# The gate projection of ten pairs of blocks with seven block products in place of eight, in a hybrid encoder block on one core

## The chip, the cores and the metric

The kernel runs on one core of a Trainium2 chip. The core has five engines with a queue of instructions each: TensorE (PE, matrix products, with its weight loads shown apart as PEld), VectorE (DVE), ScalarE (ACT), GpSimd (POOL) and SyncE (SP), which here only starts transfers. Each engine works through its queue in order, and semaphores hold an instruction back until what it needs is there. The metric is the time of one launch on the device in microseconds.

## The reference, cut to what matters

A layer mixes tokens (stick-breaking attention beside gated linear attention) and then applies a gated MLP. The change lies in the MLP. All of it is float32, for 512 tokens (SEQ), width 1024 (D) and inner width 2816 (FF):

```python
hn = _rmsnorm(h, norm_ffn_pre[l])
up = hn @ w_ffn_up[l]
act = jax.nn.gelu(_causal_dwconv(up, conv_w[l], conv_b[l]), approximate=True)
ffn = (act * (hn @ w_ffn_gate[l])) @ w_ffn_down[l]
h = h + _rmsnorm(ffn, norm_ffn_post[l])
```

The convolution goes over three tokens, one filter for each inner channel.

## The kernel before, in words

A float32 product is made of three passes: each operand is split into a high part (rounded to the float32r type that PE takes) and a low part (what is left), and PE adds high by high, high by low and low by high in PSUM. ACT makes the high part with a cast (L89 for weights, L137 elsewhere), and the low part is a subtraction, on POOL for weights of the projections (L90, in `load_w`) and on DVE elsewhere (L138, in `split`).

The normalised input of the MLP lies transposed in SBUF as `h2h` and `h2l` (high and low), eight tiles of 128 channels by 514 tokens; L207 makes the last low part. The inner width is 22 blocks of 128 (m), taken in eleven pairs p. For each block:

- the up projection: SP loads a 512 KB block of weights (`raw_up`) into one of three buffers with the tag raw, ACT casts, POOL subtracts, and PE runs 48 matmuls of 256 or 258 columns (L110, in `proj`) into `pt_up`;
- the convolution: ACT scales (L946), DVE adds the two other taps, a large and a tiny instruction for each (L949, L950), ACT applies gelu (L951);
- the gate projection: a load, a cast and a subtraction like those of up, then 24 matmuls of 512 columns (L958) into `ga`; for the first two blocks 48 of 256;
- the multiplication of the two, DVE (L961, and L963 for the odd block).

The down projection afterwards is a 2 x 2 block product done with seven products (p1, p5, p6, p3, p7, p4, p2, each 66 matmuls of 512 columns, L1020, in `product`). Its left operands are blocks of the MLP's inner activations, the half of blocks with even m and the half with odd m, each in two halves of 256 tokens: A11 and A12 are the even and the odd block for the first half of the tokens, and so on, and S1 to S4 are their sums and differences. DVE makes them at the end of each pair (L965 to L970). A11 and S1 are split at once, into `A11` and `S1`; S2, A12, A22, S4 and S3 are kept in float32 in `As` and split only when a product needs them (`late_split`, tile names `sh_p`, `sl_p`). The right operands are weights: `raw_p` for the first chunks of p1, `tw` (to which DVE adds `raw_t` and then `tv` while p1, p5 and p6 run, L1041) and `tv`. Their loads are on SP's queue.

The order on each engine is not written out: the source gives each instruction a rank, a scheduler that simulates the time line puts the instructions in order at build time, and `issue_after` pins a few of them. Buffers come free when their last reader is done.

Of the kernel before, what the change touches and what calls it, by code (L numbers as in the profile page):

```python
# [50 lines left out]
def block_kernel(ctx: ExitStack, tc: tile.TileContext, x, meta_tokens, norm_mix_pre, w_in, w_gk_up, b_gk,  # L51
# [884 lines left out]
    with tc.tile_pool(name="pu", bufs=2) as pu:  # L936
        for m in range(FT):
            pt = proj(load_w(cols(w_up, m * P), KT, f"up{m}", into=wx if m % 2 else None), h2h, h2l, FFNS, f"up{m}", apart=m < 2)
            if m % 2 == 0:
                yp = pu.tile([P, 3, HT], F32, tag="yp", name=f"yp{m}", bufs=1)  # L940
                y = yp[:, 0:2, :].rearrange("p s t -> p (s t)")
                dst = y
            else:
                y = pu.tile([P, SEQ], F32, tag="y", name=f"cy{m}", bufs=1)
                dst = As[:, A12 : A22 + 1, m // 2, :]
# [5 lines left out]
            last_gelu = act.activation(y, y, AF.Gelu_apprx_tanh)  # L951
# [8 lines left out]
            if m % 2 == 0:  # L960
                dve.tensor_tensor(out=dst, in0=pg_, in1=y, op=ALU.mult)  # L961
# [210 lines left out]
```

## Time and profile before

| | us |
|---|---|
| median of three runs | 971.16 (970.26 to 971.66) |
| profiled execution, its time | 969.08 |
| profiled execution, its span | 967.3 |
| MLP, up and gate (first up matmul 604.58, first down matmul 850.46) | 245.9 |
| down (850.46 to the end of the span) | 116.8 |

A row of a timeline has the start and the duration in us, the engine, the line, the operation, output<-inputs and the shape. A row of a group has the line, the engine, the shapes and a count, then the busy time in us and the mean of one in ns, then the idle time in front of these instructions and what ended it. Matmul durations overlap, so their pace is read from starts. A row of stretches has the length, then for each engine the busy time and the number of instructions (PE, PEld, DVE, ACT, POOL), the granted clock of PE, the share of the DMA engines' time and GB/s.

### The profile page before, as it was taken

What the parts mean: (1) busy time and instruction counts of PE and PEld (TensorE: products, weight loads), DVE (VectorE), ACT (ScalarE), POOL (GpSimd) and SP (SyncE); (2) the same over time, 40 slices, a digit from 0 to 9 for tenths busy, and PEclk for the clock granted to TensorE, in tenths of its full rate; (3) what the DMA queues carried; (4) which work ended last, traced back from release to release, by engine and by line L of the source; (5) the groups of instructions that cost most, each with busy time, mean ns of one, the idle gap of its engine ahead of it and who ended that gap; (6) DMA issues with size and microseconds to landing.
All of it is one profiled execution on the core that took longest, in us unless ns stands there. A gap on an engine that the chain in (4) does not pass through costs nothing.

```text
span 967.3 us, 16621 instructions
## 1 busy us (share of the span) xinstructions
PE 938.5 (97%) x6588; PEld 866.3 (90%) x6588; DVE 661.5 (68%) x1110; ACT 488.9 (51%) x913; POOL 357.6 (37%) x268
## 2 busy tenths in 40 slices
...
GB/s 216 45 66 66 66 45 66 66 66 44 67 66 67 86 68 45 65 88 58 75 55 90 117 207 140 61 112 93 89 92 104 87 88 94 103 237 167 254 86 127
DMA packets 129727, 92.79 MB, mean 96 GB/s; under 512 B 4064, under 2 KB 114914, under 8 KB 129650
## 3 DMA queue, kind: packets, MB, share of 16 engines
...
## 4 chain that ended last, share of the span: by engine, by line
PE 83%; DVE 10%; issue 2%; ACT 2%; POOL 2%; DMA 1%; DVEq 0%; ACTq 0%; POOLq 0%
PE pt_up L110 13%; PE ga L958 13%; PE pt_gr L110 5%; PE pt_gv L110 5%; PE pt_go L110 4%; PE pt_mg L110 4%; PE dA L1020 3%; PE pt_ms L110 3%; PE dD L1020 3%; PE pt_gk L110 2%; PE dB L1020 2%; PE wo L892 2%; PE pt_gq L110 2%; PE pt_sv L110 2%; PE pt_sk L110 2%
## 5 line engine op out<-in xcount | busy, mean ns | idle before, releaser
L90 POOL TENSOR_TENSOR wl_up<-raw_up,wh_up 128x1024 fp32r<-128x1024 f32 x22 | 53.0, 2409 | 68.3 <-ACT wh_up L89 68.3
L90 POOL TENSOR_TENSOR wl_ga<-raw_ga,wh_ga 128x1024 fp32r<-128x1024 f32 x22 | 55.2, 2509 | 56.6 <-ACT wh_ga L89 56.6
L110 PE MATMUL pt_up<-h2l,wh_up 128*128 128x256 f32 (+1 forms) x352 | 73.6, 283 | 0.3 <-DVE h2l L207 0.2
L110 PE MATMUL pt_up<-h2h,wh_up 128*128 128x256 f32 (+1 forms) x352 | 73.6, 283 | 0.2
L110 PE MATMUL pt_up<-h2h,wl_up 128*128 128x256 f32 (+1 forms) x352 | 73.3, 282 | 0.0
L958 PE MATMUL ga<-h2h,wl_ga 128*128 128x512 f32 (+1 forms) x192 | 72.2, 376 | 0.0
L958 PE MATMUL ga<-h2l,wh_ga 128*128 128x512 f32 (+1 forms) x192 | 72.2, 376 | 0.0
L958 PE MATMUL ga<-h2h,wh_ga 128*128 128x512 f32 (+1 forms) x192 | 72.0, 375 | 0.0
L89 ACT CAST wh_up<-raw_up 128x1024 fp32r<-128x1024 f32 x22 | 23.0, 1049 | 85.8 <-PE pt_up L110 76.2
L110 PEld LDWEIGHTS pt_up<-h2h,wh_up 128*128 128x128 f32 x352 | 56.9, 189 | 2.2 <-ACT h2h L206 0.5
L110 PEld LDWEIGHTS pt_up<-h2l,wh_up 128*128 128x128 f32 x352 | 55.5, 189 | 0.7 <-DVE h2l L207 0.7
L110 PEld LDWEIGHTS pt_up<-h2h,wl_up 128*128 128x128 f32 x352 | 55.3, 189 | 0.0
L958 PEld LDWEIGHTS ga<-h2h,wl_ga 128*128 128x128 f32 x192 | 36.2, 189 | 7.0
L949 DVE SCALAR_TENSOR_TENSOR cy<-pt_up,cw,cy 128x511 f32<-128x511 f32 (+1 forms) x22 | 16.4, 745 | 37.7 <-ACT cy L946 37.7
L958 PEld LDWEIGHTS ga<-h2l,wh_ga 128*128 128x128 f32 x192 | 36.2, 188 | 6.2
L958 PEld LDWEIGHTS ga<-h2h,wh_ga 128*128 128x128 f32 x192 | 36.2, 189 | 6.1
L949 DVE SCALAR_TENSOR_TENSOR yp<-pt_up,cw,yp 128x511 f32<-128x511 f32 (+1 forms) x22 | 16.4, 745 | 30.9 <-ACT yp L946 30.9
L89 ACT CAST wh_ga<-raw_ga 128x1024 fp32r<-128x1024 f32 x22 | 23.0, 1048 | 25.3 <-PE ga L958 24.8
L1048 POOL DMA_DIRECT2D tv<-in_w_ffn_down_dram x6 | 7.1, 1183 | 68.1 <-DVE wl_p L138 68.1
L90 POOL TENSOR_TENSOR wl_gr<-raw_gr,wh_gr 128x1024 fp32r<-128x1024 f32 x8 | 19.0, 2372 | 35.9 <-ACT wh_gr L89 33.1
L137 ACT CAST sh_p<-As 128x512 fp32r<-128x512 f32 (+1 forms) x30 | 17.4, 583 | 29.3 <-PE dB L1020 12.5
L90 POOL TENSOR_TENSOR wl_gv<-raw_gv,wh_gv 128x1024 fp32r<-128x1024 f32 x7 | 16.9, 2416 | 38.0 <-ACT wh_gv L89 38.0
...
## 6 DMA issues: line engine op xcount, KB each, us to landing
raw_up<-in_w_ffn_up_dram SPq DMA_DIRECT2D x22, 512.0 KB, 3.9
raw_ga<-in_w_ffn_gate_dram SPq DMA_DIRECT2D x22, 512.0 KB, 3.8
raw_t<-in_w_ffn_down_dram SPq DMA_DIRECT2D x10, 512.0 KB, 7.3
raw_gv<-in_w_in_dram SPq DMA_DIRECT2D x8, 512.0 KB, 3.9
raw_gr<-in_w_in_dram SPq DMA_DIRECT2D x8, 512.0 KB, 3.9
raw_mg<-in_w_in_dram SPq DMA_DIRECT2D x8, 512.0 KB, 3.9
raw_go<-in_w_gla_out_dram SPq DMA_DIRECT2D x8, 512.0 KB, 4.1
raw_ms<-in_w_in_dram SPq DMA_DIRECT2D x8, 512.0 KB, 4.0
```

Of the source, the lines that this page charges most:

```text
L89: act.copy(hi_out, raw)
L90: lo_eng.tensor_tensor(out=lo_out, in0=raw, in1=f32(hi_out), op=ALU.subtract)
L110: pe.matmul(dst, a[:, k, :], b[:, k, lo:hi], start=n == 0, stop=n == len(steps) - 1)
L137: act.copy(hi, src)
L892: pe.matmul(d0[i], m[k][:, t], w, start=k == 0 and q == 0, stop=k == 7 and q == 2)
L949: dve.scalar_tensor_tensor(out=y[:, d:], in0=pt[:, : SEQ - d], scalar=c, in1=y[:, d:], op0=ALU.mult, op1=ALU.add)
L958: pe.matmul(pg_[:, lo:hi], a[:, k, :], b[:, k, lo:hi], start=lo == 0 and k == 0 and q == 0, stop=k == KT - 1 and q == 2, skip_group_check= ...
L1020: mm[i] = pe.matmul(dsts[i], a, b, start=first and k == 0 and j == 0, stop=last and k == NP - 1 and j == 2, skip_group_check=True)
L1048: return lambda n, q, nk: pool.dma_start(out=t[:, q : q + nk, :], in_=block(s, c, q, nk), accum_op=ALU.add)
```

## The change

Pairs 1 to 10 no longer compute two gate blocks of 24 matmuls of 512 columns. The pair's gate product, 256 output channels by 512 tokens over 1024 input channels, is taken as a 2 x 2 by 2 x 2 block product with seven products of 12 matmuls of 256 columns (`times`, L1032). Four of the right operands are sums of quarters of h2 (`G`), computed once after pair 0 and split; three are quarters of h2. The left operands are quarters of the weights (l11, l21, l12, l22) and four sums of them (t1 to t4, `total`, L1052, on DVE). A pair's weights now come as two loads of 512 KB, each with both blocks for half of the input channels, into the raw buffers, which the sums and the splits of the quarters read. The seven splits are casts of 128x512 on ACT (L1023) and subtractions (L1024), five on DVE and two (l11, l12) on POOL.

The products are accumulated in three quarters of PSUM: a, e and g. Two of them are used for more than one sum, so e gets p1 added in place by DVE (L1067) after product t2, and ACT keeps copies (p1 L1062, u2 L1068, r5 L1071). DVE then forms two differences (d2, L1075 and L1080) and the two multiplications (L1079, L1081). Pair 0 is done as before.

The operands A12, A22 and S4 are no longer kept in SBUF: each pair's are written to HBM (`asd`) from ACT's queue, and read back into `back` (three loads of 1.44 MB) on SP's queue in the down stage. `hb` moves to another pool. The convolution and the operands go into functions with the same work in them.

```diff
-    pf = p3.enter_context(tc.tile_pool(name="pf", bufs=1))
-    hb = pf.tile([P, 4, D], F32, name="hb")
     dr = ctx.enter_context(tc.tile_pool(name="dr", bufs=1, space=bass.MemoryType.DRAM))
     hbd = dr.tile([4, P, D], F32, name="hbd")
+    asd = dr.tile([P, 3, FT // 2, SEQ // 2], F32, name="asd")
...
-    S2, A12, A22, S4, S3 = range(5)
-    As = pq.tile([P, 5, NP, HT], F32, name="As")
+    S2, S3 = range(2)
+    As = pq.tile([P, 2, NP, HT], F32, name="As")
...
+    pg = p3.enter_context(tc.tile_pool(name="pg", bufs=1, side="right"))
+    G = pg.tile([P, 4, 2, KH, HT], F32R, name="G")
...
+        def operands(p, yp, ys):
+
+            dve.tensor_tensor(out=yp[:, 2, :], in0=yp[:, 1, :], in1=ys[:, 1, :], op=ALU.subtract)
+            for o, i in ((A11, 0), (S1, 2)):
+                split(o[:, 0, p, :], o[:, 1, p, :], yp[:, i, :])
+            dve.tensor_tensor(out=As[:, S3, p, :], in0=yp[:, 0, :], in1=yp[:, 1, :], op=ALU.subtract)
+            dve.tensor_tensor(out=As[:, S2, p, :], in0=yp[:, 2, :], in1=yp[:, 0, :], op=ALU.subtract)
+            dve.tensor_tensor(out=ys[:, 2, :], in0=As[:, S2, p, :], in1=ys[:, 0, :], op=ALU.add)
+            act.dma_start(asd[:, :, p, :], ys)
...
-            for lo, hi in ((0, 256), (256, 512)) if m < 2 else ((0, 512),):
+            for lo, hi in ((0, 256), (256, 512)):
                 for k in range(KT):
                     for q, (a, b) in enumerate(((wh, h2h), (wh, h2l), (wl, h2h))):
                         pe.matmul(pg_[:, lo:hi], a[:, k, :], b[:, k, lo:hi], start=lo == 0 and k == 0 and q == 0,
                                   stop=k == KT - 1 and q == 2, skip_group_check=True)
-            if m % 2 == 0:
-                dve.tensor_tensor(out=dst, in0=pg_, in1=y, op=ALU.mult)
-                continue
-            dve.tensor_tensor(out=dst, in0=pg_.rearrange("p (s t) -> p s t", s=2), in1=y.rearrange("p (s t) -> p s t", s=2), op=ALU.mult)
-            p = m // 2
-            dve.tensor_tensor(out=yp[:, 2, :], in0=yp[:, 1, :], in1=As[:, A22, p, :], op=ALU.subtract)
-            for o, i in ((A11, 0), (S1, 2)):
-                split(o[:, 0, p, :], o[:, 1, p, :], yp[:, i, :])
-            dve.tensor_tensor(out=As[:, S3, p, :], in0=yp[:, 0, :], in1=yp[:, 1, :], op=ALU.subtract)
-            dve.tensor_tensor(out=As[:, S2, p, :], in0=yp[:, 2, :], in1=yp[:, 0, :], op=ALU.subtract)
-            dve.tensor_tensor(out=As[:, S4, p, :], in0=As[:, S2, p, :], in1=As[:, A12, p, :], op=ALU.add)
+            dve.tensor_tensor(out=y, in0=pg_, in1=y, op=ALU.mult)
+        operands(0, yp, ys)
...
+        K1, K2, N1, N2 = slice(0, KH), slice(KH, KT), slice(0, HT), slice(HT, SEQ)
+        with tc.tile_pool(name="py", bufs=1, reuse_waits="tile") as py:
+
+            def both(k, n, nm):
+                t = py.tile([P, KH, HT], F32, name=f"r{nm}")
+                dve.tensor_tensor(out=t, in0=f32(h2h[:, k, n]), in1=f32(h2l[:, k, n]), op=ALU.add)
+                return t
+
+            r12, r22 = both(K1, N2, "12"), both(K2, N2, "22")
+            dve.tensor_tensor(out=r22, in0=r12, in1=r22, op=ALU.subtract)
+            split(G[:, 0, 0], G[:, 0, 1], r22)
+            r11 = both(K1, N1, "11")
+            dve.tensor_tensor(out=r22, in0=r22, in1=r11, op=ALU.subtract)
+            split(G[:, 1, 0], G[:, 1, 1], r22)
+            dve.tensor_tensor(out=r12, in0=r11, in1=r12, op=ALU.subtract)
+            split(G[:, 2, 0], G[:, 2, 1], r12)
+            r21 = both(K2, N1, "21")
+            dve.tensor_tensor(out=r21, in0=r22, in1=r21, op=ALU.add)
+            split(G[:, 3, 0], G[:, 3, 1], r21)
+
...
+        def in_parts(src, nm, lo_eng=dve):
+
+            if place[1] == 0:
+                home, n = ((wx, 2), (wx, 2), (pt_, 1))[place[2] % 3]
+                place[2] += 1
+                place[0] = [home.tile([P, 2, KH, P], F32R, tag=t, name=f"{t}_{nm}", bufs=n) for t in ("wh", "wl")]
+            hi, lo = (t[:, place[1]] for t in place[0])
+            place[1] = 1 - place[1]
+            act.copy(hi, src)
+            lo_eng.tensor_tensor(out=lo, in0=src, in1=f32(hi), op=ALU.subtract)
+            return hi, lo
...
+        for p in range(1, NP):
+            c = slice(2 * p * P, 2 * p * P + 2 * P)
+            raw = []
+            for k in range(2):
+                r = wp.tile([P, KH, 2 * P], F32, tag="raw", name=f"raw_ga{p}_{k}")
+                sp.dma_start(r, w_gate[k * KH * P : (k + 1) * KH * P, c].rearrange("(k p) m -> p k m", p=P))
+                raw.append(r)
+            l11, l21, l12, l22 = (r[:, :, i * P : i * P + P] for r in raw for i in range(2))
+
+            def total(nm, a, b):
+                t = pt_.tile([P, KH, P], F32, tag=nm, name=f"{nm}_{p}")
+                dve.tensor_tensor(out=t, in0=a, in1=b, op=ALU.add)
+                return t
+
+            one = pst(f"ga{p}", "z")
+            two = pst(f"gb{p}", "s")
+            a, e, g = one[:, :HT], one[:, HT:], two[:, :HT]
+            yp, ys = places(p)
+            times(a, in_parts(l11, f"l11_{p}", pool), *gain_of(K1, N1), True, False)
+            kept = pu.tile([P, 3, HT], F32, tag="kept", name=f"kept{p}")
+            p1, u2, r5 = (kept[:, i, :] for i in range(3))
+            act.copy(p1, a)
+            t1 = total("t1", l11, l21)
+            t2 = total("t2", t1, l22)
+            times(e, in_parts(t2, f"t2_{p}"), *summed(1), False, False)
+
+            dve.tensor_tensor(out=e, in0=e, in1=p1, op=ALU.add)
+            act.copy(u2, e)
+            conv(2 * p, flat(yp))
+            times(g, in_parts(t1, f"t1_{p}"), *summed(0), True, False)
+            act.copy(r5, g)
+            times(e, in_parts(total("t3", l22, l21), f"t3_{p}"), *summed(2), False, False)
+            times(a, in_parts(l12, f"l12_{p}", pool), *gain_of(K2, N1), False, True)
+            d2 = pu.tile([P, 2, HT], F32, tag="d2", name=f"d2_{p}")
+            dve.tensor_tensor(out=d2[:, 1, :], in0=r5, in1=e, op=ALU.subtract)
+            last_gelu = conv(2 * p + 1, flat(ys))
+            times(e, in_parts(total("t4", t2, l12), f"t4_{p}"), *gain_of(K2, N2), False, True)
+            times(g, in_parts(l22, f"l22_{p}"), *summed(3), False, True)
+            dve.tensor_tensor(out=flat(yp), in0=one, in1=flat(yp), op=ALU.mult)
+            dve.tensor_tensor(out=d2[:, 0, :], in0=g, in1=u2, op=ALU.subtract)
+            dve.tensor_tensor(out=flat(ys), in0=flat(d2), in1=flat(ys), op=ALU.mult)
+            operands(p, yp, ys)
...
+        back = pd.tile([P, 3, NP, HT], F32, name="back")
+        A12, A22, S4 = (back[:, i] for i in range(3))
...
         for q, nk in CH:
             sp.dma_start(tv[:, q : q + nk, :], block(1, R, q, nk))
+        for i in (2, 1, 0):
+            sp.dma_start(back[:, i], asd[:, i])
```

How the instructions move. On PE, at the start of the second pair's gate (the names are tiles with a number; `pt_up` is an up block, `ga` and `gb` are the gate's PSUM, `wh` and `wl` are weights' high and low parts), before:

```order
4140 L110 MATMUL pt_up_7604<-h2l,wh_up_7600 128x258
4141 L110 MATMUL pt_up_7604<-h2h,wl_up_7601 128x256
4142 L110 MATMUL pt_up_7604<-h2h,wl_up_7601 128x258
4143 L958 MATMUL ga_7666<-h2h,wh_ga_7662 128x512
4144 L958 MATMUL ga_7666<-h2l,wh_ga_7662 128x512
4145 L958 MATMUL ga_7666<-h2h,wl_ga_7663 128x512
4146 L958 MATMUL ga_7666<-h2h,wh_ga_7662 128x512
```

and now:

```order
4141 L110 MATMUL pt_up_7680<-h2h,wl_up_7677 128x256
4142 L110 MATMUL pt_up_7680<-h2h,wl_up_7677 128x258
4143 L1032 MATMUL ga_7632<-h2h,wh_l_1_7636 128x256
4144 L1032 MATMUL ga_7632<-h2l,wh_l_1_7636 128x256
4145 L1032 MATMUL ga_7632<-h2h,wl_l_1_7637 128x256
```

The same queue 57 rows on, where the second up block ends and the products with sums begin:

```order
4202 L110 MATMUL pt_up_7792<-h2h,wl_up_7789 128x258
4203 L1032 MATMUL gb_7633<-G,wh_t_1_7735 128x256 x2
4204 L1032 MATMUL ga_7632<-G,wh_l_1_7636 128x256 x2
4205 L1032 MATMUL gb_7633<-G,wl_t_1_7736 128x256
4206 L1032 MATMUL gb_7633<-G,wh_t_1_7735 128x256 x2
4207 L1032 MATMUL gb_7633<-G,wl_t_1_7736 128x256
4208 L1032 MATMUL gb_7633<-G,wh_t_1_7735 128x256 x2
4209 L1032 MATMUL gb_7633<-G,wl_t_1_7736 128x256
4210 L1032 MATMUL gb_7633<-G,wh_t_1_7735 128x256 x2
```

The one block of 24 products of 512 columns has become products of 256 columns, which begin with l11 right behind the first up block; the second up block (pt_up_7792) now comes before t1 and t2, and these two alternate.

On DVE, from the last low part of h2 to the first pair's operands (`r` are quarters of h2 put together, `G` the low parts of their sums, `yp` and `ys` the activations of an even and an odd block), before:

```order
777 L207 TENSOR_TENSOR h2l<-ygh_0_7325,h2h 128x4x128
778 L949 SCALAR_TENSOR_TENSOR yp_7409<-pt_up_7360,cw,yp_7409 128x511
779 L950 SCALAR_TENSOR_TENSOR yp_7409<-pt_up_7360,cw,yp_7409 128x1
780 L949 SCALAR_TENSOR_TENSOR yp_7409<-pt_up_7360,cw,yp_7409 128x510
781 L950 SCALAR_TENSOR_TENSOR yp_7409<-pt_up_7360,cw,yp_7409 128x2
782 L949 SCALAR_TENSOR_TENSOR cy_7527<-pt_up_7478,cw,cy_7527 128x511
783 L950 SCALAR_TENSOR_TENSOR cy_7527<-pt_up_7478,cw,cy_7527 128x1
784 L961 TENSOR_TENSOR yp_7409<-ga_7422,yp_7409 128x512
```

and now:

```order
777 L207 TENSOR_TENSOR h2l<-ygh_0_7323,h2h 128x4x128
778 L997 TENSOR_TENSOR r_7604<-h2h,h2l 128x1024
779 L997 TENSOR_TENSOR r_7606<-h2h,h2l 128x1024
780 L997 TENSOR_TENSOR r_7611<-h2h,h2l 128x1024
781 L997 TENSOR_TENSOR r_7619<-h2h,h2l 128x1024
782 L1001 TENSOR_TENSOR r_7606<-r_7604,r_7606 128x1024
783 L951 SCALAR_TENSOR_TENSOR yp_7356<-pt_up_7364,cw,yp_7356 128x511
784 L952 SCALAR_TENSOR_TENSOR yp_7356<-pt_up_7364,cw,yp_7356 128x1
785 L1006 TENSOR_TENSOR r_7604<-r_7611,r_7604 128x1024
786 L951 SCALAR_TENSOR_TENSOR yp_7356<-pt_up_7364,cw,yp_7356 128x510
787 L952 SCALAR_TENSOR_TENSOR yp_7356<-pt_up_7364,cw,yp_7356 128x2
788 L138 TENSOR_TENSOR G<-r_7606,G 128x1024
```

The four quarters and the first sums stand between h2 and the convolution of the first block. The other sums and low parts follow among the convolutions and operands of pair 0, then seven weight sums and four low parts, up to the first correction of e:

```order
818 L1052 TENSOR_TENSOR t_2_8013<-raw_ga_1_7893,raw_ga_0_7891 128x512
819 L951 SCALAR_TENSOR_TENSOR ys_7635<-pt_up_7792,cw,ys_7635 128x510
820 L1024 TENSOR_TENSOR wl_l_1_7769<-t_1_7847,wh_l_1_7768 128x512
821 L952 SCALAR_TENSOR_TENSOR ys_7635<-pt_up_7792,cw,ys_7635 128x2
822 L1052 TENSOR_TENSOR t_2_7917<-t_2_7915,raw_ga_1_7893 128x512
823 L951 SCALAR_TENSOR_TENSOR yp_7634<-pt_up_7680,cw,yp_7634 128x510
824 L1067 TENSOR_TENSOR ga_7632<-ga_7632,kept_7652 128x256
825 L952 SCALAR_TENSOR_TENSOR yp_7634<-pt_up_7680,cw,yp_7634 128x2
826 L1024 TENSOR_TENSOR wl_l_1_7864<-raw_ga_1_7630,wh_l_1_7863 128x512
```

Row 824 is that correction of pair 1 (L1067). It stands behind all the rows shown and those between.

At the end of the MLP, ACT's queue before:

```order
768 L137 CAST S_7350<-yp_9417 128x256
769 L1071 DMA g3bc<-in_norm_ffn_post_dram 128x1024
770 L137 CAST wh_p_9625<-raw_p_9576 128x1024
771 L137 CAST sh_p_9805<-As 128x512
772 L137 CAST sh_p_9826<-As 128x512
```

and now:

```order
862 L137 CAST S_7348<-yp_9993 128x256
863 L972 DMA asd<-ys_9994 384x1x256
864 L1186 DMA g3bc<-in_norm_ffn_post_dram 128x1024
865 L137 CAST wh_p_10317<-raw_p_10268 128x1024
866 L137 CAST sh_p_10500<-As 128x512
```

The write of the last pair's three operands stands ahead of the cast of p1's weights (`wh_p`). On SP's queue in the same place, before:

```order
143 L1073 DMA tw<-in_w_ffn_down_dram 128x2x512
144 L993 DMA raw_t_9629<-in_w_ffn_down_dram 128x2x512
145 L993 DMA raw_t_9648<-in_w_ffn_down_dram 128x2x512
146 L993 DMA raw_t_9667<-in_w_ffn_down_dram 128x2x512
147 L993 DMA raw_t_9686<-in_w_ffn_down_dram 128x512
148 L993 DMA raw_t_9929<-in_w_ffn_down_dram 128x2x512
149 L1103 DMA tv<-in_w_ffn_down_dram 128x2x512 x5
150 L1103 DMA tv<-in_w_ffn_down_dram 128x512
```

and now:

```order
143 L1188 DMA tw<-in_w_ffn_down_dram 128x2x512
144 L1220 DMA back<-asd 128x2816
145 L1108 DMA raw_t_10321<-in_w_ffn_down_dram 128x2x512
146 L1220 DMA back<-asd 128x2816 x2
147 L1108 DMA raw_t_10340<-in_w_ffn_down_dram 128x2x512
148 L1108 DMA raw_t_10359<-in_w_ffn_down_dram 128x2x512
149 L1218 DMA tv<-in_w_ffn_down_dram 128x2x512 x2
150 L1108 DMA raw_t_10378<-in_w_ffn_down_dram 128x512
151 L1218 DMA tv<-in_w_ffn_down_dram 128x2x512 x3
152 L1218 DMA tv<-in_w_ffn_down_dram 128x512
```

Behind the loads of `tw` the first read of `back` stands ahead of the first further `raw_t`, and the other two ahead of all later ones and of `tv`.

More of the change, by code (lines that the diff above doesn't have):

```diff
@@ L930, in block_kernel, with conv, conv_gelu @@
     pq = ctx.enter_context(tc.tile_pool(name="pq", bufs=1, side="right"))
-    S2, A12, A22, S4, S3 = range(5)
-    As = pq.tile([P, 5, NP, HT], F32, name="As")
+    S2, S3 = range(2)
+    As = pq.tile([P, 2, NP, HT], F32, name="As")
     A11 = pq.tile([P, 2, NP, HT], F32R, tag="first", name="A11")
     S1 = pq.tile([P, 2, NP, HT], F32R, tag="second", name="S1")
-    with tc.tile_pool(name="pu", bufs=2) as pu:
-        for m in range(FT):
-            pt = proj(load_w(cols(w_up, m * P), KT, f"up{m}", into=wx if m % 2 else None), h2h, h2l, FFNS, f"up{m}", apart=m < 2)
-            if m % 2 == 0:
[L940 to L945, printed above, removed]
+    KH = KT // 2
+    pg = p3.enter_context(tc.tile_pool(name="pg", bufs=1, side="right"))
+    G = pg.tile([P, 4, 2, KH, HT], F32R, name="G")
+    with tc.tile_pool(name="pu", bufs=1, reuse_waits="tile") as pu:
+        ctx_t = ExitStack()
+        def conv(m, y):
+            return conv_gelu(m, proj(load_w(cols(w_up, m * P), KT, f"up{m}"), h2h, h2l, FFNS, f"up{m}"), y)
+        def conv_gelu(m, pt, y):
             act.activation(y, pt[:, 0:SEQ], AF.Identity, scale=cw[:, 2, m : m + 1], bias=cw[:, 3, m : m + 1])
@@ L950, in block_kernel, with places, flat @@
                 dve.scalar_tensor_tensor(out=y[:, :d], in0=pt[:, TQ - d :], scalar=c, in1=y[:, :d], op0=ALU.mult, op1=ALU.add)
-            last_gelu = act.activation(y, y, AF.Gelu_apprx_tanh)
-            with tc.issue_after(late.ins) if m < 2 else ExitStack():
+            return act.activation(y, y, AF.Gelu_apprx_tanh)
+        def places(p):
+            yp = pu.tile([P, 3, HT], F32, tag="yp", name=f"yp{p}")
+            ys = pu.tile([P, 3, HT], F32, tag="ys", name=f"ys{p}", bufs=2)
+            return yp, ys
+        def flat(t):
+            return t[:, 0:2, :].rearrange("p s t -> p (s t)")
+        def operands(p, yp, ys):
[6 more added lines that the diff above has]
+            act.dma_start(asd[:, :, p, :], ys)
+        yp, ys = places(0)
+        for m in range(2):
+            pt = proj(load_w(cols(w_up, m * P), KT, f"up{m}", into=wx if m % 2 else None), h2h, h2l, FFNS, f"up{m}", apart=True)
+            y = flat((yp, ys)[m])
+            conv_gelu(m, pt, y)
+            with tc.issue_after(late.ins):
                 wh, wl = load_w(cols(w_gate, m * P), KT, f"ga{m}", into=wx if m % 2 else None)
             pg_ = pst(f"ga{m}", "z")
-            for lo, hi in ((0, 256), (256, 512)) if m < 2 else ((0, 512),):
+            for lo, hi in ((0, 256), (256, 512)):
                 for k in range(KT):
@@ new lines, in block_kernel @@
+        pt_ = ctx_t.enter_context(tc.tile_pool(name="pt_", bufs=1, reuse_waits="tile"))
+        place = [None, 0, 0]
+        def in_parts(src, nm, lo_eng=dve):
[8 more added lines that the diff above has]
+            return hi, lo
```

20 lines of the change are left out of this document (16 added, 4 removed).

## Prediction

> **What bounds the kernel now.** I read the page's busy shares and its chain first, then the FFN stage by stretches of one pair of blocks, then the groups of DVE in that stage, then the rows in order of time at the three places that the change touches: where pair 1 begins, a steady pair, and the start of the down product.
>
> ```profile
> PE 938.5 (97%) x6588; PEld 866.3 (90%) x6588; DVE 661.5 (68%) x1110; ACT 488.9 (51%) x913; POOL 357.6 (37%) x268
> PE 83%; DVE 10%; issue 2%; ACT 2%; POOL 2%; DMA 1%; DVEq 0%; ACTq 0%; POOLq 0%
> 646.70:669.30 22.60, 22.60 (x146) 20.49 (x145) 11.25 (x16) 7.51 (x11) 9.89 (x4) 1.00 0.32 92
> 691.90:714.50 22.60, 22.60 (x145) 20.54 (x144) 11.25 (x16) 7.56 (x10) 9.89 (x4) 1.00 0.32 92
> ```
>
> The last two rows are the busy time in two steady pairs (in order PE, PEld, DVE, ACT, POOL, then granted clock, DMA share and GB/s). PE works through all 22.60 us, DVE half of it, POOL 9.89, the clock is whole. So a matmul less is time less here, as long as the others still arrive in time.
>
> **Fewer products.** Consecutive starts give the pace of each width:
>
> ```profile
> 703.22 0.40 PE L110 MATMUL pt_up<-h2h,wh_up 128*128 128x256 f32 x2
> 708.98 0.39 PE L958 MATMUL ga<-h2h,wh_ga 128*128 128x512 f32 x1
> 711.99 0.40 PE L958 MATMUL ga<-h2l,wh_ga 128*128 128x512 f32 x1
> 604.78 0.28 PE L110 MATMUL pt_up<-h2l,wh_up 128*128 128x256 f32 x1
> 606.69 0.28 PE L110 MATMUL pt_up<-h2h,wl_up 128*128 128x256 f32 x1
> ```
>
> From 708.98 to 711.99 are 13 matmuls of 512 columns, 0.2315 us each; from 604.78 to 606.69 are 16 of 256, 0.1194 us each. An up block takes 708.98 - 703.22 = 5.76 us. The gate of a pair was 48 x 0.2315 = 11.11 us and becomes 7 x 12 x 0.1194 = 10.03: 1.08 us less a pair, **-10.8 us** over ten. The gain is small since an eighth fewer products pays 3% more for each column. [...] Every other term is a delay; I see no second gain, since POOL's two fewer gate splits shorten nothing that PE waits for.
>
> **The first pair.** Before pair 1 can use its sums, DVE must make four sums of h2. Its work and prices:
>
> ```profile
> 612.08 0.68 DVE L207 TENSOR_TENSOR h2l<-ygh,h2h 128x512 fp32r<-128x512 f32 x1
> L138 DVE TENSOR_TENSOR wl_p<-raw_p,wh_p 128x1024 fp32r<-128x1024 f32 x2 | 2.4, 1222 | 2.2 <-ACT wh_p L137 2.2
> L138 DVE TENSOR_TENSOR sl_p<-As,sh_p 128x512 fp32r<-128x512 f32 x25 | 17.1, 685 | 4.9 <-ACT sh_p L137 4.9
> L949 DVE SCALAR_TENSOR_TENSOR yp<-pt_up,cw,yp 128x511 f32<-128x511 f32 (+1 forms) x20 | 14.9, 745 | 23.9 <-ACT yp L946 23.9
> L950 DVE SCALAR_TENSOR_TENSOR yp<-pt_up,cw,yp 128x1 f32<-128x1 f32 (+1 forms) x20 | 4.2, 209 | 0.0
> L961 DVE TENSOR_TENSOR yp<-ga,yp 128x512 f32<-128x512 f32 x11 | 7.6, 691 | 23.8 <-PE ga L958 22.7 <-ACT yp L951 1.1
> L970 DVE TENSOR_TENSOR As<-As 128x256 f32<-128x256 f32 x10 | 4.1, 412 | 0.0
> 623.96 0.40 PE L110 MATMUL pt_up<-h2h,wh_up 128*128 128x256 f32 x2
> ```
>
> h2 is whole at 612.76. In DVE's new order there stand ahead of pair 1's first correction (the add of p1 into e, on which t3's product waits): twelve instructions of 128x1024 (four quarters put together, four sums, four low parts), 14.6 us at 1.22; four convolutions of up blocks, 4 x 2 x (0.745 + 0.209) = 7.6; pair 0's two multiplications, 1.4, and its six small operand steps, 2.5; eleven sums and low parts of weights of 128x512, 7.5 at 0.685. That is 33.6 us, so 646.4 if DVE never waits. PE starts pair 1 at 623.96. Two up blocks and one product of 12 matmuls later (2 x 5.76 + 1.43) it is 636.9; t1's, t2's and the next pair's first product bring it to 641.2, and there t3 needs that correction and a copy by ACT (its cast of 128x256 takes 0.41). 646.4 + 0.4 + 0.5 = 647.3: a wait of about 6 us. Before, the same stretch had none. It is the lower estimate, as POOL holds DVE up:
>
> ```profile
> 704.36 2.53 POOL L90 TENSOR_TENSOR wl_ga<-raw_ga,wh_ga 128x1024 fp32r<-128x1024 f32 x1 [3.17 <-ACT wh_ga L89]
> 704.65 2.51 DVE L138 TENSOR_TENSOR A<-yp,A 128x256 fp32r<-128x256 f32 x1
> L138 DVE TENSOR_TENSOR A<-yp,A 128x256 fp32r<-128x256 f32 x11 | 25.5, 2320 | 0.2
> L138 DVE TENSOR_TENSOR S<-yp,S 128x256 fp32r<-128x256 f32 x10 | 4.1, 413 | 0.0
> L969 DVE TENSOR_TENSOR As<-yp 128x256 f32<-128x256 f32 x10 | 23.0, 2300 | 0.3
> L90 POOL TENSOR_TENSOR wl_up<-raw_up,wh_up 128x1024 fp32r<-128x1024 f32 x22 | 53.0, 2409 | 68.3 <-ACT wh_up L89 68.3
> ```
>
> The low part of A takes 2320 ns and that of S, the same shape, 413; the slow one starts 0.29 us after a POOL subtraction and ends with it. L969 against L970 reads the same. L949, which reads PSUM, stays at 745 whatever POOL does. So a DVE step with both inputs in SBUF that meets a POOL subtraction waits it out. In the first stretch nearly all new DVE steps are such, and POOL has two up splits (2.41 each) and two half splits (1.2, half of 2.41): up to 7.2 us more, of which I take 3. Next in line, the raw buffers: pair 2's up weights can only be loaded when DVE has made the last low part of pair 1's weights, and then come a load, a cast and POOL's split,
>
> ```profile
> raw_up<-in_w_ffn_up_dram SPq DMA_DIRECT2D x22, 512.0 KB, 3.9
> L89 ACT CAST wh_up<-raw_up 128x1024 fp32r<-128x1024 f32 x22 | 23.0, 1049 | 85.8 <-PE pt_up L110 76.2
> 540.00:560.00 20.00, 16.23 (x66) 12.37 (x65) 19.96 (x25) 4.40 (x5) 8.68 (x5) 0.91 0.38 121
> ```
>
> 3.9 + 1.05 + 2.41 = 7.4 us, of which PE's remaining gate products of the pair (t4 and l22 and the next first ones, three to four of 1.43) cover all but about 2. The last row is a stretch in which PE now waits 3.77 us in all: the clock fell to 0.91, 1.8 us of work, so a long wait may cost more than itself. The place is bounded by 4 (sums finish early, pair 0's steps let them pass) and 15 (6 + 7.2 + 2); I take **+10**.
>
> **The steady pairs.** Without collisions DVE had 4 x (0.745 + 0.209) + 2 x 0.69 + 6 x 0.42 = 7.7 us a pair; 11.25 is what it shows, so 3.5 us was POOL. Now come four weight sums and five low parts (9 x 0.685 = 6.2), and the additions in PSUM and differences (about 1.3): 15.2 us, 9.4 of it with both inputs in SBUF. POOL has 2 x 2.41 + 2 x 1.2 = 7.2. If all of POOL's time falls on DVE, it needs 22.4 us of a pair that should last 22.60 - 1.08 = 21.5; if half of it does, 18.8. That half is nearest to today's 3.5 of 9.89 with SBUF steps of 2.5, but a fuller DVE is hit more often. Between, DVE keeps up on the mean, yet it works in order, and t3 waits for one step of it: PE has 24 up matmuls and t1's product between t2's last and t3's first (2.9 + 1.4 = 4.3 us), and the add and the copy need 0.9, so one POOL subtraction in front is borne and a second one is not. The three raw buffers are now freed by DVE's last low part and not by POOL, and the round (that part, load 3.9, cast, split 2.41, the next load, DVE's sums up to the next add) fills about all of two pairs. Bounds 0 and 15 (10 times 0.9 from the mean, and 0.6 from stragglers); I take **+4**. The operands' writes to HBM ride on ACT's queue (three blocks, 0.4 MB a pair) beside a DMA share of 0.32: nothing, unless that queue stops behind a DVE step, which is the next place.
>
> **The down stage.** Three operands are read back there, 4.3 MB.
>
> ```profile
> 850.46 0.40 PE L1020 MATMUL dA<-wh_p,A 128*128 128x512 f32 x1
> 852.36 1.05 ACT L137 CAST wh_p<-raw_p 128x1024 fp32r<-128x1024 f32 x1
> 853.50 1.23 DVE L138 TENSOR_TENSOR wl_p<-raw_p,wh_p 128x1024 fp32r<-128x1024 f32 x1 [0.38 <-issue]
> 854.75 13.28 SPq L993 DMA_DIRECT2D raw_t<-in_w_ffn_down_dram  x5
> 855.00:860.00 5.00, 5.00 (x24) 4.08 (x23) 3.20 (x4) 1.60 (x2) 0.00 (x0) 1.00 1.02 367
> 860.00:865.00 5.00, 5.00 (x24) 4.12 (x23) 4.86 (x5) 2.73 (x4) 0.00 (x0) 1.00 1.05 382
> 874.71 1.23 DVE L1041 TENSOR_TENSOR tw<-tw,tv 128x1024 f32<-128x1024 f32 x1 [1.22 <-DMA tv<-in_w_ffn_down_dram]
> ```
>
> Down starts at 850.46. p1's third chunk of weights is cast at 852.36 and its low part done at 854.73, 4.3 us after the start and 1.3 before PE wants it (5.6 in, 24 matmuls). In the new order ACT has the last pair's write ahead of that cast, and the write waits for S4, the last DVE step of the pair, about 5.1 us after the last product (two multiplications, six steps). Cast, DVE and handovers make it 8.1: **+2** (0 to 3). Behind it SP's queue: the three reads stand ahead of two weight loads for p5 and of all of tv, the last of them waiting for that write. At 367 to 382 GB/s, where the DMA engines are already full, 4.3 MB takes about 11 us. The weights it pushes were awaited with little slack: DVE waits 1.22 us for tv today. p5 and p6 cover most: **+3** (2 to 5).
>
> **Sum** against the profiled execution, whose span is 967.3 us and whose time is 969.08, 2.1 under the median of 971.16: -10.8 + 10 + 4 + 5 = +8.2. I take 7.5, as the raw buffers are counted in two of these; on the median 978.7 us.
>
> **The rivals.** *Faster*: the delays stay at their lower ends, 4 + 0 + 2, and the sum is -4.8: 966.4 us. For it speaks that PE has up blocks to turn to and POOL has less to do than before; against it that DVE's 33.6 us stand in one line in front of pair 1. It decides at the steady pair: at 21.5 us each it is this one. *DVE and POOL become the bound*: every POOL subtraction falls on a DVE step, a pair needs 22.4 us and stragglers, and t3 waits each time: -10.8 + 10 + 15 + 5 = +19, 990 us. The rows at 704.36 and 704.65 speak for it, 18.8 us at half collisions against. [...] *A wash*: the delays together come to 9 to 13 us, 971 us.
>
> **How the numbers follow.** 0.2%, 1.9 us, is about what a measurement of this kernel can tell from none. My forecast (974 to 984) 0.42, the bound by DVE and POOL 0.18, faster 0.32, the wash 0.08. Below 965 and above 990 I leave out 2 in 10, from the faster case's tail (gain whole) and the bound's: 965 to 990. The forecast's own range is 974 to 984. Faster 0.32, same 0.08, slower 0.60.
>
> **What would show it.** Right: a wait of PE of 5 to 10 us about 640 to 650 with DVE busy all through; steady pairs of 21.5 to 22.2 us and DVE steps of 2 us and more in each; the first down product with a wait of 2 us for a low part about 6 us in, and a wait in p5 or p6. Wrong: pairs of 21.5 with no wait of PE before t3 and no wait at pair 1 (faster), or pairs above 22.6 (the bound by DVE). A 256-column pace that isn't 0.119 us would change the first term.

## The result and the profile after

The changed kernel takes 982.14 us (median; 980.12 to 984.2) beside 970.71 for the kernel before (967.89 to 971.66), a ratio of 1.0123 with a 95% interval of 1.0091 to 1.0155: 11.4 us slower. The forecast was 978.7, with a range of 965 to 990.

The page of the changed kernel, its busy shares and its chain:

```profile
PE 939.0 (96%) x6948; PEld 883.5 (90%) x6948; DVE 713.8 (73%) x1242; ACT 519.6 (53%) x997; POOL 346.5 (35%) x268
PE 62%; DVE 19%; DMA 8%; issue 4%; POOL 3%; ACT 3%; SPq 0%; DVEq 0%; POOLq 0%; ACTq 0%
```

PE's share of the chain falls from 83% to 62%; DVE takes 19% and transfers 8%. PE's busy time has not fallen, though ten pairs run fewer columns: a matmul in a stretch of low clock is longer (two of 256 columns at 652.03 have 0.63 us, at 656.00, with the clock whole, 0.40), so the profiled times are not a count of work.

Cut into three, by the first up matmul of pair 1, the first matmul of down and the first of p3, the two traces read (us; all later kernels are cut the same way):

| | pairs 1 to 10 | p1, p5, p6 | rest |
|---|---|---|---|
| before | 623.96 to 850.46: 226.50 | to 896.30: 45.84 | 71.00 |
| changed | 626.29 to 853.80: 227.51 | to 910.03: 56.23 | 71.47 |

Ten pairs are 1.0 longer, p1, p5 and p6 10.4, the rest 0.5: 11.9 us, and the medians differ by 11.4. The 2.3 us by which the MLP's second pair starts later in this trace lie ahead of the change: the first up matmul of the MLP starts at 596.00 before and at 598.65 now (the table ahead of the prediction puts it at 604.58, a later one), while the change's first new step (a quarter of h2 put together, on DVE) comes at 615.07. In the twelve traces of this document that first matmul starts anywhere from 594.60 to 600.15, so I don't count the 2.3 us.

In the first stretch, PE's timeline with its waits (the first is for a part of t2, the last in front of t3's product), the correction of e on DVE's timeline, and the stretches (span; PE, PEld, DVE, ACT, POOL busy; granted clock, DMA share, GB/s):

```profile
641.84 0.52 PE L1032 MATMUL ga<-G,wh_l 128*128 128x256 f32 x2 [1.29 <-ACT wh_l L1023]
645.09 0.39 PE L1032 MATMUL ga<-G,wl_l 128*128 128x256 f32 x1 [1.55 <-DVE wl_l L1024]
647.18 0.51 PE L1032 MATMUL gb<-G,wh_l 128*128 128x256 f32 x2 [0.63 <-ACT wh_l L1023]
649.46 0.39 PE L1032 MATMUL ga<-h2h,wl_l 128*128 128x256 f32 x1 [1.26 <-POOL wl_l L1024]
651.41 0.61 PE L1032 MATMUL ga<-G,wh_t 128*128 128x256 f32 x2 [0.48 <-ACT kept L1068]
650.54 0.42 DVE L1067 TENSOR_TENSOR ga<-ga,kept 128x256 f32<-128x256 f32 x1
641.00:651.00 10.00, 5.63 (x36) 4.60 (x36) 10.00 (x20) 4.14 (x9) 5.11 (x2) 1.00 0.31 98
651.00:655.00 4.00, 3.59 (x17) 3.59 (x18) 1.33 (x4) 2.55 (x5) 0.53 (x1) 0.58 0.85 246
681.40:724.87 43.47, 43.29 (x362) 43.08 (x361) 28.01 (x57) 20.29 (x36) 16.18 (x8) 1.00 0.41 116
```

DVE is busy through all of 641 to 651 while PE waits for one part of a weight after another; then the clock is 0.58. The last row is two steady pairs: PE is busy 43.29 of 43.47 us and DVE 28.01, so the steady pair lasts 21.73 us.

At the start of down, PE's waits, ACT's queue in front of the late cast, SP's issues, and stretches of this kernel:

```profile
862.09 0.73 PE L1135 MATMUL dA<-wh_p,A 128*128 128x512 f32 x2 [2.53 <-ACT wh_p L137]
885.08 0.49 PE L1135 MATMUL dD<-wh_p,S 128*128 128x512 f32 x1 [1.98 <-ACT wh_p L137]
858.47 0.41 ACT L137 CAST S<-yp 128x256 fp32r<-128x256 f32 x1
859.70 0.52 ACTq L972 DMA_DIRECT2D asd<-ys  x1
860.99 1.04 ACT L137 CAST wh_p<-raw_p 128x1024 fp32r<-128x1024 f32 x1 [2.11 <-DMA tw<-in_w_ffn_down_dram]
868.72 1.06 SPq L1220 DMA_DIRECT2D back<-asd  x2
869.88 0.91 SPq L1108 DMA_DIRECT2D raw_t<-in_w_ffn_down_dram  x2
862.00:866.00 4.00, 3.39 (x8) 2.45 (x9) 3.94 (x5) 2.97 (x5) 0.00 (x0) 0.66 1.04 369
880.00:891.00 11.00, 7.99 (x26) 5.76 (x26) 8.39 (x9) 3.59 (x4) 0.00 (x0) 0.84 1.03 381
892.00:894.00 2.00, 2.00 (x10) 1.65 (x10) 2.00 (x3) 0.24 (x2) 0.00 (x0) 1.00 1.06 390
```

and one of the kernel before:

```profile
880.00:885.00 5.00, 5.00 (x23) 4.07 (x22) 5.00 (x6) 4.19 (x6) 0.00 (x0) 1.00 0.46 170
```

The write of asd goes out at 859.70 and the cast behind it begins at 860.99. The wait named in front of the cast is for a load of tw, whose weights this cast doesn't read; its source, raw_p, was issued at 837.67, long before, so the name is of the last event seen and says little. The reads of back are issued at 867 to 869, and from 870 the DMA engines are full for some 24 us (1.01 over 870 to 880, 1.03 up to 891, still 1.06 at 892 to 894), where in the kernel before they are down to 0.46 at 880 to 885; PE waits for p5's weights at 885 and the clock is 0.84.

### The profile page after: what moved, and what is told of

The parts are those of the page before. It is cut to its first block, busy times and chain, and to the rows that moved or that the text cites. A ratio compares the mean times of both kernels' runs of the same rounds, so it can differ in the third digit from the quotient of the medians.

```text
span 981.5 us, 17617 instructions
## 1 busy us (share of the span) xinstructions
PE 939.0 (96%) x6948; PEld 883.5 (90%) x6948; DVE 713.8 (73%) x1242; ACT 519.6 (53%) x997; POOL 346.5 (35%) x268
## 4 chain that ended last, share of the span: by engine, by line
PE 62%; DVE 19%; DMA 8%; issue 4%; POOL 3%; ACT 3%; SPq 0%; DVEq 0%; POOLq 0%; ACTq 0%
PE pt_gr L110 5%; PE pt_gv L110 5%; PE pt_go L110 4%; PE pt_mg L110 4%; PE pt_up L110 4%; PE pt_ms L110 3%; DMA raw_up<-in_w_ffn_up_dram 3%; DMA raw_ga<-in_w_ffn_gate_dram 3%; PE pt_gk L110 2%; PE pt_sv L110 2%; PE dB L1135 2%; PE pt_gq L110 2%; PE dD L1135 2%; PE ga L1032 2%; DVE acc L779 2%
## 5 line engine op out<-in xcount | busy, mean ns | idle before, releaser
L1024 POOL TENSOR_TENSOR wl_l<-raw_ga,wh_l 128x512 fp32r<-128x512 f32 x15 | 31.4, 2095 | 37.0 <-ACT wh_l L1023 27.0
L1052 DVE TENSOR_TENSOR t<-raw_ga 128x512 f32<-128x512 f32 x10 | 13.1, 1308 | 40.6 <-DMA raw_ga<-in_w_ffn_gate_dram 40.6
L1024 DVE TENSOR_TENSOR wl_t<-t,wh_t 128x512 fp32r<-128x512 f32 x30 | 26.8, 917 | 3.5 <-ACT wh_t L1023 3.5
L110 PE MATMUL pt_gv<-hnh,wl_gv 128*128 128x272 f32 (+1 forms) x128 | 27.6, 289 | 0.1
L110 PE MATMUL pt_mg<-hnl,wh_mg 128*128 128x258 f32 (+1 forms) x128 | 27.6, 286 | 0.0
L110 PE MATMUL pt_gr<-hnh,wl_gr 128*128 128x258 f32 (+1 forms) x128 | 27.6, 292 | 0.0
L137 ACT CAST wh_p<-tw 128x1024 fp32r<-128x1024 f32 (+1 forms) x21 | 20.0, 967 | 13.9 <-DVE tw L1156 8.4
L110 PE MATMUL pt_gr<-hnl,wh_gr 128*128 128x258 f32 (+1 forms) x128 | 27.4, 290 | 0.0
L110 PE MATMUL pt_go<-oh,wh_go 128*128 128x258 f32 (+1 forms) x128 | 27.0, 285 | 0.0
L90 POOL TENSOR_TENSOR wl_mg<-raw_mg,wh_mg 128x1024 fp32r<-128x1024 f32 x8 | 19.8, 2478 | 20.4 <-ACT wh_mg L89 20.3
L110 PE MATMUL pt_go<-oh,wl_go 128*128 128x258 f32 (+1 forms) x128 | 27.0, 283 | 0.0
## 6 DMA issues: line engine op xcount, KB each, us to landing
back<-asd SPq DMA_DIRECT2D x3, 1408.0 KB, 10.6
```

Source lines behind the costliest of these rows:

```text
L90: lo_eng.tensor_tensor(out=lo_out, in0=raw, in1=f32(hi_out), op=ALU.subtract)
L110: pe.matmul(dst, a[:, k, :], b[:, k, lo:hi], start=n == 0, stop=n == len(steps) - 1)
L137: act.copy(hi, src)
L1024: lo_eng.tensor_tensor(out=lo, in0=src, in1=f32(hi), op=ALU.subtract)
L1052: dve.tensor_tensor(out=t, in0=a, in1=b, op=ALU.add)
```

## The experiments

The theory after the first trace: the gate itself gains what was forecast, and gives it back where pair 1 begins; what makes the kernel slower is putting the operands aside, by two separate causes, the write on ACT's queue and the reads on SP's. The rivals are in the expectations.

**The reads behind tv's loads.**

```diff
-            sp.dma_start(tv[:, q : q + nk, :], block(1, R, q, nk))
-        for i in (2, 1, 0):
-            sp.dma_start(back[:, i], asd[:, i])
+            last_tv = sp.dma_start(tv[:, q : q + nk, :], block(1, R, q, nk))
+        with tc.issue_after(last_tv.ins):
+            for i in (2, 1, 0):
+                sp.dma_start(back[:, i], asd[:, i])
```

> Theory: the three reads of back are what makes p5 wait (2.0 and 0.9 us, and a clock of 0.84 after it), since they stand ahead of raw_t and tv on SP's queue. Behind the last tv load these waits go: the down stage falls from 127.7 us to about 122 to 124 and the time from 982 to 977 or 978. Rival: the reads have to be made anyway, and the wait only moves to p3, which needs S4 first; then p6 or p3 shows a wait of 2 us or more and the time stays at 981 to 983.

977.12 us (973.93 to 979.92), 1.0062 of before (1.0045 to 1.0079), as the theory had it. p1, p5 and p6 take 51.79 us; the waits in p5 are gone and no new one comes in p3 (the rest takes 71.85).

**The last write on POOL's queue.**

```diff
-            act.dma_start(asd[:, :, p, :], ys)
+            (pool if p == NP - 1 else act).dma_start(asd[:, :, p, :], ys)
```

> Only the last pair's write to asd goes from ACT's queue to POOL's. Theory: it held the cast of p1's third chunk of weights back; without it the waits of 2.5 and 0.5 us in p1 and the clock of 0.66 behind them go, the down stage falls from 127.7 to about 122 to 124 and the time to 977 or 978. Rival: the cast waits for something else on that queue (the load of g3bc that stands between, or the pair's late S1); then the wait stays at over 2 us and the time at 981 to 983.

982.58 us, 1.0129 (1.0114 to 1.0143): no gain. The time is the rival's, but not its reason: the wait in p1 fell from 2.53 to 0.37 us, and p5's doubled, on PE's timeline of this kernel:

```profile
856.15 0.73 PE L1135 MATMUL dA<-wh_p,A 128*128 128x512 f32 x2 [0.37 <-ACT wh_p L137]
881.19 0.80 PE L1135 MATMUL dD<-wh_p,S 128*128 128x512 f32 x1 [4.00 <-ACT wh_p L137]
883.61 0.79 PE L1135 MATMUL dD<-wl_p,S 128*128 128x512 f32 x1 [1.62 <-DVE wl_p L138]
862.00:888.00 26.00, 19.22 (x72) 14.05 (x71) 15.72 (x14) 7.89 (x10) 0.00 (x0) 0.87 0.97 373
```

p1 came through earlier and then waited for weights whose transfer had not become any earlier: p1, p5 and p6 take 58.05 us.

**Both edits.**

> Both edits together. Theory: two separate causes, so the gains add up: the down stage at 117 to 119 us (before: 116.8), no wait of PE in p1 and p5, time 971 to 973. Rival: one cause behind the other, so that both together bring no more than the better of the two, 977.

972.29 us (970.19 to 975.88), 1.0020 (1.0009 to 1.0031): the theory's time, but the gains don't add up, 5.0 us and nothing alone and 9.9 together. p1, p5 and p6 take 47.48, 1.6 over before. In p1 two short waits are left (0.36 and 0.52 us) and in p5 none:

```profile
857.72 0.74 PE L1135 MATMUL dA<-wh_p,A 128*128 128x512 f32 x2 [0.36 <-ACT wh_p L137]
858.98 0.50 PE L1135 MATMUL dA<-wl_p,A 128*128 128x512 f32 x1 [0.52 <-DVE wl_p L138]
```

In the traces too the write costs 4.3 us (51.79 - 47.48) when the reads are out of the way and nothing while they are there, and the reads alone cost 12.2 us (58.05 - 45.84), more than the whole difference of 10.4.

**The sums of h2 left out.** The products take plain quarters of h2 where they took G. The edit drops the block that makes G (L994 to L1010), and

```diff
-            return G[:, i, 0], G[:, i, 1]
+            return gain_of((K1, K2)[i % 2], (N1, N2)[i // 2])
```

> The four sums of h2 are left out: the products take plain quarters of h2 in their place, so twelve DVE steps of 128x1024 and four casts are missing, PE's work is the same. Theory: the line of DVE work in front of pair 1 is what makes PE wait; pairs 1 and 2 go from 53.7 us to 44 to 47, the time from 982 to 973 to 976. Rival: pair 1 waits for its weights (the two loads, the sums t1 to t4 and the three raw buffers), and the sums of h2 are covered by pair 0; then pairs 1 and 2 stay over 51 us and the time over 979.

974.05 us (972.25 to 977.0), 1.0040 (1.0025 to 1.0056): 8.1 us less than the changed kernel, as the theory had it. Pairs 1 to 10 take 220.09 us in place of 227.51, and pairs 1 and 2 of them 46.9 (625.59 to 672.53) in place of 53.7. The line of DVE work is the cause of most of the delay at pair 1. A wait of 2.10 us is left there, with low clock behind it (the last section has both).

**Pair 1 as pair 0.** The loop over the plain blocks runs to m = 3, with 24 matmuls of 512 columns from m = 2 on, and the products' loop begins with pair 2.

```diff
-            for lo, hi in ((0, 256), (256, 512)):
+            for lo, hi in ((0, 256), (256, 512)) if m < 2 else ((0, 512),):
...
-        for p in range(1, NP):
+        for p in range(2, NP):
```

> Pair 1 is done as pair 0 is, with 24 matmuls of 512 columns a block; products begin with pair 2, nine pairs of them. Nothing is left out. Theory: the line of 33.6 us on DVE then ends, with pair 1's own 7.7 us, at about 654, before pair 2's t3 at about 664, so PE waits nowhere in pairs 1 to 3: the MLP falls by 9 to 10 us for 1.08 us more of PE work, time 972 to 974 (down as in the changed kernel). Rival: the wait belongs to the first pair of products whichever it is (its loads, the raw buffers); then it only moves a pair on, and the time is 981 to 984.

979.17 us (977.6 to 982.36), 1.0101 (1.0084 to 1.0119): only 3 us of the 8 to 10 expected. The waits in front of the products are gone, but one has come that I hadn't seen:

```profile
635.14 0.47 PE L987 MATMUL ga<-h2h,wh_ga 128*128 128x512 f32 x1 [3.79 <-DVE yp L989]
625.13 2.64 DVE L138 TENSOR_TENSOR G<-r,G 128x1024 fp32r<-128x1024 f32 x1
628.48 2.63 DVE L138 TENSOR_TENSOR G<-r,G 128x1024 fp32r<-128x1024 f32 x1
631.03 3.36 DVE L1006 TENSOR_TENSOR r<-r,r 128x1024 f32<-128x1024 f32 x1
634.31 0.68 DVE L989 TENSOR_TENSOR yp<-ga,yp 128x512 f32<-128x512 f32 x1
```

L989 is pair 0's first multiplication. It reads the gate's PSUM buffer, which pair 1's first gate block needs, and it stands on DVE behind two low parts and a sum of h2, which take 2.64, 2.63 and 3.36 us where a step of that size takes 1.22 alone.

**The three edits together.**

> The edits of the two experiments on the down stage and pair 1 done as before, together. Theory: what is left is the gain of nine pairs, 9.7 us, less about 1.5 in the steady pairs and 1.6 in the down stage: 963 to 966, faster than both kernels. Rival: the gain of the products is not there once nothing waits (the steady pairs already stand at 21.7 us because DVE lets them), and the time is that of the kernel before, 969 to 972.

970.89 us (967.46 to 973.08), 1.0002 (0.9986 to 1.0017): the time the rival gave, but not its reason. The same wait of 3.79 us stands at 635 with a clock of 0.69 over 631 to 640.

**All low parts from pair 2 on by DVE**, otherwise as the previous one.

```diff
-            times(a, in_parts(l11, f"l11_{p}", pool), *gain_of(K1, N1), True, False)
+            times(a, in_parts(l11, f"l11_{p}"), *gain_of(K1, N1), True, False)
```

The same is done for l12, and `load_w` of the up blocks gets `lo_eng=dve`.

> As the previous experiment, and all low parts of up and gate weights from pair 2 on are made by DVE, none by POOL. DVE's own work a pair rises by about 2 x 1.22 + 2 x 0.685 = 3.8 us, POOL's falls to 0, and no step meets a POOL subtraction. Theory now: DVE has room (14.0 of 21.7 us a pair in the changed kernel), so the pairs stay at 21.6 to 21.8 us and the time within 1.5 us of the previous one. Rival, my prediction's other case: DVE is close to being the bound and each added step comes in front of t3; then the pairs go to over 22.3 us and the time 6 us or more above the previous one.

968.91 us (966.12 to 971.65), 0.9991 (0.9979 to 1.0004), 2.0 under the previous one. DVE has room. In the traces two steady pairs take 43.01 us (703.78 to 746.79) where they took 43.49 (703.98 to 747.47), so a little seems to be won by having no POOL subtraction beside DVE; the intervals of the two times overlap, so the times alone don't show it.

**Only the operands put aside**, all gates plain.

> Only the third part of the change on the kernel before: A12, A22 and S4 are put aside in HBM and read back, with queues as the changed kernel has them; all gate blocks are 24 matmuls of 512 columns. Theory: the down stage is slowed by the write and the reads alone, whatever the gate does; p1, p5 and p6 take 54 to 57 us (before 45.8) and the time is 979 to 982. Rival: it is slowed because the last pair of products ends with a longer DVE tail; then p1, p5 and p6 take under 50 us and the time is 971 to 975.

981.27 us (980.94 to 981.93), 1.0120 (1.0103 to 1.0137), the theory's time. Pairs 1 to 10 take 226.51 us as before, p1, p5 and p6 57.76, a little over the theory's 57 and 11.9 over before. p1 has no wait here, since the plain pair's operands are done sooner (the last write goes out 2.7 us after the first matmul of down, in the changed kernel 5.9); p5 has four (1.21, 0.76, 2.50 and 0.86). This one part costs as much as the whole change.

**Pair 0's multiplication first.** Beside the edits of the experiment with all low parts on DVE, the sums are held behind it:

```diff
-            dve.tensor_tensor(out=r22, in0=r22, in1=r11, op=ALU.subtract)
+            with tc.issue_after(first_mult.ins):
+                dve.tensor_tensor(out=r22, in0=r22, in1=r11, op=ALU.subtract)
```

The next split and the next subtraction (r12) are held likewise.

> As the previous combination (reads late, last write on POOL's queue, pair 1 plain, low parts on DVE), and pair 0's first multiplication stands on DVE ahead of the last three sums of h2, where it stood behind two low parts and a sum. That multiplication frees the gate's PSUM buffer. Theory: the wait of 3.8 us at 635 in the combination, with a granted clock of 0.69 in the 9 us around it, comes from this order alone, so both go: 6 to 7 us less, 961 to 964 us, faster than the kernel before by 6 to 9 us. Rival: DVE's whole line of work up to about 650 is what is late, so the wait only moves to pair 1's next gate or to pair 2's first products and the time stays within 2 us of 969.

966.21 us (964.43 to 970.66), 0.9966 (0.9951 to 0.9981). The wait at 635 is gone and 2.7 of the 6 to 7 us are won, but another wait of 3.10 us stands at 651, so the rival was right for the rest: PE waits for the convolution of block 2 (its PSUM buffer), whose steps stand on DVE behind a low part of up weights and among three of gate weights.

```profile
650.94 0.48 PE L110 MATMUL pt_up<-h2h,wh_up 128*128 128x256 f32 x2 [3.10 <-DVE yp L952]
```

**That convolution ahead of low parts.** The low parts of pair 2's gate weights are held behind it, and in the same way that of block 5's up weights (in `load_w`); five of them stood ahead of it or among its steps.

```diff
-            lo_eng.tensor_tensor(out=lo, in0=src, in1=f32(hi), op=ALU.subtract)
+            with tc.issue_after(taps[2].ins) if nm.endswith("_2") else ExitStack():
+                lo_eng.tensor_tensor(out=lo, in0=src, in1=f32(hi), op=ALU.subtract)
```

> As the previous kernel, and on DVE the convolution of block 2 stands ahead of the low part of block 5's up weights and of four low parts of pair 2's gate weights, where it stood behind or between them. The convolution frees the PSUM buffer of the next up block; PE waited 3.1 us for it at 651. Theory: DVE reaches it 2 to 3 us earlier, the wait falls under 0.5 us, and the time by 2.5 to 3.5 us, to 963 to 964. Rival: DVE's total work before pair 2 is what is late, so the same wait turns up a step later, in front of pair 2's first products or its t3 (over 2 us), and the time stays within 1 us of 966.

963.40 us (960.88 to 964.28), 0.9925 (0.9912 to 0.9939): 6.9 us faster than the kernel before and 18.7 faster than the change as it was given. Pairs 1 to 10 take 217.01 us, and PE has no wait over 0.5 us in them. Two stretches of this kernel, one up to the time at which pair 2 has begun (its first up matmul is at 647.91) and one of two steady pairs:

```profile
608.00:650.00 42.00, 41.76 (x303) 39.25 (x302) 37.60 (x54) 21.52 (x31) 15.02 (x6) 1.00 0.26 74
743.00:786.00 43.00, 43.00 (x362) 43.00 (x361) 33.94 (x66) 20.42 (x36) 0.00 (x0) 1.00 0.40 117
```

DVE is now busy 33.94 of 43.00 us and PE still all of it. All ten, by the three cuts (us; the fourth number is the median time):

| kernel | pairs 1 to 10 | p1, p5, p6 | rest | time |
|---|---|---|---|---|
| reads late | 226.77 | 51.79 | 71.85 | 977.12 |
| last write on POOL | 227.39 | 58.05 | 70.72 | 982.58 |
| both | 227.21 | 47.48 | 70.72 | 972.29 |
| no sums | 220.09 | 54.68 | 72.24 | 974.05 |
| pair 1 plain | 224.05 | 55.63 | 72.67 | 979.17 |
| three edits | 224.53 | 49.68 | 70.79 | 970.89 |
| low parts on DVE | 222.98 | 48.22 | 71.11 | 968.91 |
| aside only | 226.51 | 57.76 | 71.84 | 981.27 |
| multiplication first | 219.55 | 48.58 | 71.21 | 966.21 |
| convolution first | 217.01 | 48.00 | 71.11 | 963.40 |

## Why the prediction was right, and where it was not

**Fewer products, -10.8.** Right. In the last kernel nine pairs of products bring 226.50 - 217.01 = 9.5 us, and nine times 1.08 is 9.7. The steady pair there is 21.5 us, the forecast one.

**The first pair, +10.** Right in size, and right in that DVE's line of work is the cause; where PE would wait was wrong, and two errors in the line cancelled. From pair 1's start (626.29) to pair 3's first product (the page's timeline has it at 679.95) two pairs take 53.7 us, where 2 x 21.55 = 43.1 would do: +10.6. PE has nothing to do for 6.7 us of them, and 3.4 us at half clock cost another 1.7. Leaving out the sums takes 7.4 us off pairs 1 to 10, so that much of the 10.6 is shown to be theirs. The wait did not come in one piece in front of t3, which has 0.48 us: 4.73 us came before it, for parts of weights, 2.84 of them (1.29 and 1.55) for the parts of t2, whose sum and low part stand in that same line on DVE.

The correction of e comes at 650.54, and 646.4 with 3 us of collisions and the 2.3 by which this trace runs late gives 651.7, but that is luck in part. DVE needs less for the line than I added up, since steps in a row start sooner than their lengths say (1.13 us from the step at 634.32 to the next, with a length of 1.22). Against that, five steps that met POOL took 4.6 us more than alone, where I had 3, and 1.1 us went by until h2 was whole: POOL makes one of its low parts too (L207), which I had overlooked, and it ends at 614.09 in the kernel before, not at 612.76.

The collisions show on DVE and on POOL, whose timelines read:

```profile
617.38 3.50 DVE L997 TENSOR_TENSOR r<-h2h,h2l 128x1024 f32<-128x1024 f32 x3 [1.08 <-POOL h2l L207]
622.79 2.57 DVE L1006 TENSOR_TENSOR r<-r,r 128x1024 f32<-128x1024 f32 x1
634.32 1.22 DVE L1009 TENSOR_TENSOR r<-r,r 128x1024 f32<-128x1024 f32 x1
635.45 1.22 DVE L138 TENSOR_TENSOR G<-r,G 128x1024 fp32r<-128x1024 f32 x1
621.37 2.90 POOL L90 TENSOR_TENSOR wl_up<-raw_up,wh_up 128x1024 fp32r<-128x1024 f32 x1 [4.02 <-ACT wh_up L89]
638.53 5.95 POOL L1024 TENSOR_TENSOR wl_l<-raw_ga,wh_l 128x512 fp32r<-128x512 f32 x1 [6.68 <-issue]
```

Two like steps of DVE take 2.57 and 1.22 us; the first began during a POOL subtraction and ended 1.1 us after it. What I had one-sided is the last row: a POOL subtraction of half size, 1.2 us by my estimate, takes 5.95 while DVE is busy with 13 steps through all of 638.53 to 644.48. I had reckoned with longer steps on DVE alone.

**The steady pairs, +4.** Too much: 21.73 us over eight pairs is 1.5 us over 21.55. The step that failed is the half of POOL's time falling on DVE. A steady pair shows DVE busy 14.0 us, under the 15.2 that I had for it without any collision, and POOL 8.1 in place of 7.2: over 681.40 to 768.35 POOL's subtractions of l11 and l12 (L1024) took 1.80 us on the mean for six and 1.28 for two, where I had 1.2, and POOL has time to spare. On DVE the sum t1 (L1052) took 1.62 us there, where the other sums took 0.69. The DVE steps of 2 us and more that I had named as a sign are not there: in the two steady pairs shown the longest takes 1.73 us. The experiment with everything on DVE shows that DVE wasn't near its bound, so the rival *DVE and POOL become the bound* falls.

**The down stage, +5.** Mis-sized: 10.4 in p1, p5 and p6, and 10.9 with the rest. Both mechanisms were right, and the wrong step is the sentence that p5 and p6 cover most of the 11 us of reads. They cover almost none: the reads stand ahead of weights that came barely in time before (DVE waited 1.22 us for tv there), and half clock came on top of the waits: of the 10.4 us, PE stood still for 6.1, and two times 3.4 us at half clock (from 863.28 and from 887.17) make another 3.4. The wait in p1, too, was for the cast itself (2.53 us) and hardly for the low part (0.53), which I had named. Nor do the two terms add, as I had them: p5's weights come no earlier when the write is out of the way, so the time that PE gains in p1 it loses in p5. With the reads late the write costs 4.3, where I had 2; I had counted a wait (2.6 + 0.5 us in that kernel) without the half clock behind it (the granted clock is 0.75 over 862.50 to 867.00).

**The total.** -10.8 + 10.6 + 1.5 + 10.4 + 0.5 is 12.2, measured 11.4 in medians and 11.9 in the stretches. That the forecast's 7.5 came as near as it did is luck in part: +4 was too much by 2.5 and +5 too little by 5.4 to 5.9. *Faster* failed at the first pair, which it took at 4, and at the down stage, which it took at 2, not at the steady pair that I had named as the point of decision; that point came out near its side.

What stays open: whether the 1.6 to 3.8 us left in p1, p5 and p6 in the kernels with both edits come from the last pair's longer tail on DVE alone wasn't tried. The 3.2 us of the first pair that stay without the sums were not taken apart either.
